# A decoder layer with stick-breaking attention: meta columns in one transpose, first values as a bias, the 528-column scores halved

## The chip, the cores and the metric

The kernel runs on one core of a Trainium2 chip. A core has TensorE (PE; its weight loads are listed apart as PEld), VectorE (DVE), ScalarE (ACT), GpSimd (POOL) and SyncE (SP), whose queue issues nearly all the transfers between device memory (DRAM) and the on-chip memory SBUF. TensorE writes to PSUM, eight banks of 128 partitions by 512 float32 columns; DVE and ACT read it, POOL doesn't in this kernel. Each engine works through its own instructions in order, and the engines wait for each other by semaphores. The metric is the device time of one execution in microseconds.

## The reference

One layer over 2048 tokens and 16 meta tokens in front of them, model width 1024. Every row is normalised and multiplied with one wide weight matrix. The columns feed two kinds of attention, their gates, and a merge:

```
xn   = rms_norm(h, norm_gain)
proj = xn @ w_in            # sb_q, sb_k, sb_v, sw_q, sw_k, sw_v, sb_z, sw_z, g_sb, g_sw
# stick-breaking attention: 8 heads of 64, all earlier positions s < t
z    = q k^T / 8
log_1m = where(mask, log_sigmoid(z) - z, 0)      # log of 1 - sigmoid(z)
w    = where(mask, exp(log_sigmoid(z) + (sum of log_1m over later s)), 0)
o_sb = w v
# sliding-window attention: 16 heads in 2 groups, window 128, a sink per head
o_sw = softmax([scores, sink])[..., :-1] v
y    = sigmoid(g_sb) * ((o_sb * silu(sb_z)) @ w_branch_sb) + sigmoid(g_sw) * ((o_sw * silu(sw_z)) @ w_branch_sw)
out  = rms_norm(h + y @ w_out, final_norm_gain)[:, real tokens]
```

## The kernel before

**Precision.** The result must be that of float32. A float32 value is split in a high part (type fp32r, which TensorE multiplies in one pass) and a low part, the rest; a product is high x high, high x low, low x high, added up in PSUM. So most loops issue three matmuls per block, and the helpers `evac_split` (lines 117 to 120: ScalarE writes the high part at L119, VectorE the low part at L120) and `split` (L110 to L116) occur everywhere.

**Order.** Tokens are in reversed order, 16 blocks of 128, four groups of four blocks (512 columns), two halves: groups 2 and 3 first, then 0 and 1. For each half the kernel computes the stick-breaking q, k and v (`sb_q`, `sb_k`, `sb_v`, kept in DRAM as qd, kd, vd), runs the sliding-window attention (`window`) woven into other projections, then the stick-breaking attention (`stick`) woven into gate projections (L454 are the projections' matmuls). Last comes `finish`, with the output projections. `weave` (L140) takes turns between a main list (projections) and a side list (attention): each `yield` names a cost, and the side may spend `ratio` times what the main has spent. In `stick` the costs are 0.45 for a row, 0.43 for a turn and so on; `cost_sb` (L1388) is their sum and gives the ratio, so that both lists end together.

**Who orders what.** TensorE's instructions go out in the order of the program. The other engines' orders, SP's queue too, are laid down by a planner that simulates the engines beforehand, apart from some stretches at the start that are by hand. At run time each queue is strictly in order.

**Stick-breaking, one row of blocks (`row`, L900).** For a head h and a group g of queries, a step (n, j) takes block j of the group, with 128 queries as partitions, and up to four blocks of keys from block 4(g+n)+j on, up to the last block. Because of the reversal the weights are a running product: a sigmoid of -z by ScalarE (L920), then one scan by VectorE that multiplies along the row (L930; L928 with a mask where the diagonal lies), carried on from the row before. What is kept in a row is the remaining product before each position, so the value matmul uses differences of neighbouring values instead of values (`sb_v`, variable d), and the very first value of each block of queries comes in with weight 1.

Each row that reaches the last key also has 16 columns for the meta tokens. If it has fewer than four blocks, they fit into the same PSUM bank (tag "z", two banks). If it has four (`own`), there are 512 + 16 = 528 scores, and the 16 have a bank of their own (tag "zm", one bank): two matmuls of 512 (L916) and two of 16 (L918), for the two halves of the split q, in the order 512, 16, 512, 16; then two sigmoids (L920, L922). This happens once for each head and group, 32 times.

**Turning (`turn`, L934).** Five or six steps after a row (LT), its 128x128 blocks are transposed by TensorE into a bank "t" (L941), split into wth and wtl (L119, L120), and two steps later multiplied with the value differences vc into the output bank, tag "o", of which there is one (`values`, L967). After the last row of a group, `turn_meta` (L948) transposes the 16 meta columns of each of the four rows, one at a time, into rows 0 to 15 of "zm" (L952), and `evac_split` puts the high part into rows 0 to 15 and the low part into rows 32 to 47 of wm, a constant tile, one for each group of the half. Rows 64 on of wm hold ones at the place of the block they belong to (memset and affine_select, L859 and L860), and the rows of vm against them hold the first values. So one matmul of wm with vm (the last L967 of a group) adds meta tokens and first values. Then ScalarE copies the bank "o" to SBUF (L971) and two DMAs store the result od. Its high and low value columns are stored apart and added later.

**First values (`sb_v`, L547).** The first value of each block is copied to vf (L555); the closure `firsts` transposes eight of them (L578), splits them (L532, L533) and stores them by DMA into vm. The closure `turned` writes the meta values' differences into rows 0 to 15 of vm and copies them to rows 32 to 47 (L596).

Of the kernel before, what the change touches and what calls it, by code (L numbers as in the profile page):

```python
# [11 lines left out]
ALU = mybir.AluOpType  # L12
# [36 lines left out]
def tile_kernel(ctx, tc, x, xt, meta, metat, gain, w_in, w_sb, w_sw, w_out, sinks, fgain,  # L49
# [498 lines left out]
    def sb_v(p):  # L548

        def use(g, acc, ms):  # L550
            t, d = tmp(), tmp()
            A.copy(t, acc)
            V.tensor_tensor(d[:, :GT - 1], t[:, 1:], acc[:, :GT - 1], op=ALU.subtract)
            f0 = p % 2 * 8
            A.copy(vf[:, f0 + g % 2 * 4:f0 + g % 2 * 4 + 4], t.rearrange("p (b q) -> p b q", b=4)[:, :, 0])  # L555

            def join(nxt):
                V.tensor_tensor(d[:, GT - 1:], nxt, t[:, GT - 1:], op=ALU.subtract)
                if g % 2 == 0:
                    A.copy(vn[:, p:p + 1], t[:, 0:1])  # L560

            def rows():
                tr = ps("zm")
                for i in range(4):
                    T.transpose(tr[:, i * P:(i + 1) * P], d[:, i * P:(i + 1) * P], ident)
                hl = tr.rearrange("p (b a d) -> p a b d", b=4, a=2)
                vt = [tmp(F32R).rearrange("p (b d) -> p b d", b=4) for a in range(2)]
                for a, t in enumerate(vt):
                    A.copy(t[:, :, 0:64], hl[:, a])
                for a, t in enumerate(vt):  # L570
                    V.tensor_tensor(t[:, :, 64:128], hl[:, a], f32(t[:, :, 0:64]), op=ALU.subtract)
                for a, t in enumerate(vt):
                    DMA(vd[p][g][a], t)

            def firsts():

                tr = ps("zm")
                T.transpose(tr[:8, :P], vf[:, f0:f0 + 8], ident)  # L578
                vb = tmp(F32R)[:8, :2 * P].rearrange("p (a d) -> p a d", a=2)
                meta_rows(tr[:8, :P], vb[:, :, 0:64], vb[:, :, 64:128])  # L580
                DMA(vm[64 + 4 * g:72 + 4 * g, p], vb)

            def meta():
                mc = meta_cols(ms)
                m = tmp()
                mv, md = m[:, :NM + 1], m[:, 32:32 + NM]
                G.memset(mv[:, NM:], 0.0)
                A.copy(mv[:, :NM], mc)
                V.tensor_tensor(md, mv[:, 1:], mv[:, :NM], op=ALU.subtract)
                join(mv[:, 0:1])  # L590

                def turned():
                    tr = ps("t")
                    T.transpose(tr[:NM, :P], md, ident)
                    meta_rows(tr[:NM, :P], vm[0:NM, p, :, 0:64], vm[0:NM, p, :, 64:128])
                    A.copy(vm[32:32 + NM, p], f32(vm[0:NM, p]))  # L596
                    rows()
                soon.append(turned)

            if ms is None:  # L600
                join(vn[:, p:p + 1] if g % 2 else vf[:, f0 + 4:f0 + 5])
# [246 lines left out]
    def stick(groups, bp):  # L848
# [4 lines left out]
        for tag, shape, n in (("q1", [P, GT], 2), ("q2", [P, GT], 2), ("v", [P, 4, P], 5), ("wh", [P, GT], 3), ("wl", [P, GT], 3),  # L853
                              ("k", [P, KW], 2)):
            for _ in range(n):
                bp.tile(shape, F32R, tag=tag, name=tag, bufs=n)
        for g in groups:
            w = wm[g % 2]
            G.memset(f32(w), 1.0)  # L859
            G.affine_select(out=w, in_=f32(w), pattern=[[-1, 4], [0, P]], compare_op=ALU.is_equal, fill=0.0,  # L860
                            base=-64 - 4 * g, channel_multiplier=1)
        av_todo = []
        mask = None
        if groups[0]:
            mask = bp.tile([P, RW], F32, name="mask")
# [33 lines left out]
        def row(h, g, n, j):  # L899
# [10 lines left out]
            k0 = (b0 - 4 * groups[0]) * P  # L910
            own = end and nb == 4
            z = ps("z")
            zm = ps("zm") if own else None
            for t, qt in enumerate(st["q"]):
                lq = qt[:, j * P:(j + 1) * P]
                T.matmul(z[:, :w], lhsT=lq, rhs=kt[h][:, k0:k0 + w], start=t == 0, stop=t == 1)  # L916
                if own:
                    T.matmul(zm[:, :NM], lhsT=lq, rhs=kt[h][:, k0 + w:k0 + w + NM], start=t == 0, stop=t == 1)  # L918
            r = bp.tile([P, RW], F32, tag="row", name="row", bufs=12)
            A.activation(r[:, :w], z[:, :w], AF.Sigmoid, scale=-1.0)  # L920
            if own:
                A.activation(r[:, w:w + NM], zm[:, :NM], AF.Sigmoid, scale=-1.0)  # L922
                w += NM
            if n == 0 and mask is None:
# [6 lines left out]
            last[j] = r[:, w - 1:w]  # L931
            rows_of[h, g, n, j] = r

        def turn(h, g, n, i):  # L934
# [13 lines left out]
        def turn_meta(h, g):  # L948
            p, a = divmod(h, 2)
            tr = ps("zm")  # L950
            for j in range(4):
                T.transpose(tr[:NM, j * P:(j + 1) * P], rows_of[h, g, 3 - g, j][:, GT - P * j:GT - P * j + NM], ident)  # L952
            w = wm[g % 2]
            evac_split(w[0:NM], w[32:32 + NM], tr[:NM])
            av_todo.append((h, g, vm[:, p, a, :], w, None, False, True))

        def values():
# [10 lines left out]
            if last:  # L968
                p, a = divmod(h, 2)
                u = tmp()  # L970
                A.copy(u, o)  # L971
                for n in range(2):
# [6 lines left out]
        for s in range(n + lt + 3):  # L979
# [4 lines left out]
            if 0 <= t < n:  # L984
# [336 lines left out]
    for half, groups in enumerate(halves):  # L1321
# [61 lines left out]
        with tc.tile_pool(name=f"sb{half}", bufs=1, side="left") as bp:  # L1383
# [106 lines left out]
```

## Time and profile before

| | |
|---|---|
| median of 3 runs | 2112.88 us (2112.0 to 2113.49) |
| the profiled execution | 2112.16 us, span 2110.4 us |
| granted TensorE clock | 0.999 |
| stick-breaking stage, first half | about 374 to 590 us |
| stick-breaking stage, second half | about 1111 to 1612 us |

The profile is of one execution, in microseconds from the first instruction. Its page gives busy time by engine, the chain of work that ended last, and groups of instructions by line: out<-in by the program's names, count, busy time, mean ns of one, and the idle time of the engine just before them with what ended it. A timeline lists instructions in order: start, duration, engine, line, operation, tiles, shape, count. A matmul's listed duration holds its way through the array, so neighbours overlap; what it costs is read from the start of one to the start of the next. A shape such as 128*16 128x128 is the size of the weights and what is streamed past them.

### The profile page before, as it was taken

Reading aid. Unit: us, or ns where it says so; the run is one execution under the profiler, and the core shown is the slowest. Engines: PE = TensorE matmul, PEld = TensorE weight load, DVE = VectorE, ACT = ScalarE, POOL = GpSimd, SP = SyncE. Lnnn points to the kernel's source line nnn. Section 1 sums busy time; section 2 is a strip of 40 time slices with the busy share of each in tenths; the row PEclk is TensorE's granted clock in tenths of the full one; section 3 lists DMA queues with packets and bytes.
Section 4 is the critical chain, followed back from the end, with each engine's and each line's share of the span. In section 5 each row is a group of like instructions: output and inputs, shape, how many; then the busy total and the mean of one; then the engine's idle time right before and its main releaser. Section 6 shows DMA issues by size and latency. Waiting matters only on the chain.

```text
span 2110.4 us, 30845 instructions
## 1 busy us (share of the span) xinstructions
PE 2094.4 (99%) x10695; PEld 1755.2 (83%) x10695; DVE 1479.1 (70%) x2375; ACT 1058.8 (50%) x2438; POOL 300.1 (14%) x484
## 2 busy tenths in 40 slices
PE   9999999999999999999999999999999999999998
PEld 7888888888878888888888888888888888788887
DVE  7897986888878554887738888877774456564553
ACT  6677774555646335777735555555553202221131
POOL 2133444211000000232310000000000232000000
PEclk9999999999999999999999999999999999999999
DMA  9955545766449674435455344343424996568532
GB/s 337 324 174 193 191 168 181 238 194 200 139 142 338 232 256 155 152 136 178 137 172 153 123 126 127 118 125 95 123 88 142 360 323 203 181 232 309 160 100 90
DMA packets 169580, 391.07 MB, mean 185 GB/s; under 512 B 23601, under 2 KB 27697, under 8 KB 169425
## 3 DMA queue, kind: packets, MB, share of 16 engines
q1 hardware_dynamic: 169136, 388.84, 54.9%
q8 instruction: 85, 1.39, 0.3%
q14 instruction: 71, 0.57, 0.1%
q10 hardware_dynamic: 288, 0.27, 0.0%
HBM read 241.68 MB, written 145.18 MB: 183 GB/s over the span
## 4 chain that ended last, share of the span: by engine, by line
PE 91%; DVE 3%; ACT 3%; DMA 2%; issue 1%; SPq 0%; ACTq 0%; DVEq 0%
PE ps_g L454 39%; PE ps_o L967 6%; PE ps_z L916 6%; PE ps_t L941 6%; PE ps_z L754 3%; PE ps_o L810 2%; PE ps_g L252 1%; PE ps_g L253 1%; PE ps_g L251 1%; PE ps_z L252 1%; PE ps_z L251 1%; PE ps_z L253 1%; PE ps_t L252 1%; PE ps_t L253 1%; PE ps_t L251 1%; PE ps_t L788 1%
## 5 line engine op out<-in xcount | busy, mean ns | idle before, releaser
L454 PE MATMUL ps_g<-xh,wh 128*128 128x512 f32 x1296 | 532.1, 411 | 0.8 <-DVE tmp L675 0.5
L454 PE MATMUL ps_g<-xl,wh 128*128 128x512 f32 x1296 | 507.6, 392 | 0.4 <-DVE xl L1169 0.3
L454 PE MATMUL ps_g<-xh,wl 128*128 128x512 f32 x1296 | 507.7, 392 | 0.0
L930 DVE TENSOR_TENSOR_SCAN row<-row 128x512 f32<-128x512 f32 (+4 forms) x256 | 297.1, 1161 | 91.9 <-ACT row L920 39.5
L454 PEld LDWEIGHTS ps_g<-xh,wl 128*128 128x128 f32 x1296 | 243.3, 188 | 54.4 <-DVE wl L1217 0.4
L920 ACT ACTIVATE row<-ps_z 128x512 f32<-128x512 f32 (+1 forms) x320 | 172.4, 539 | 213.5 <-PE ps_z L916 192.3
L454 PEld LDWEIGHTS ps_g<-xh,wh 128*128 128x128 f32 x1296 | 244.3, 188 | 41.4 <-ACT xh L1168 1.0
L454 PEld LDWEIGHTS ps_g<-xl,wh 128*128 128x128 f32 x1296 | 244.8, 189 | 37.8 <-DVE xl L1169 1.7
L119 ACT ACTIVATE wth<-ps_t 128x512 fp32r<-128x512 f32 (+1 forms) x320 | 170.7, 533 | 76.3 <-PE ps_t L941 75.2
L120 DVE SCALAR_TENSOR_TENSOR wtl<-ps_t,wth 128x512 fp32r<-128x512 f32 (+1 forms) x320 | 188.9, 590 | 25.3 <-ACT wth L119 24.8
L916 PE MATMUL ps_z<-kt,q 128*128 128x512 f32 (+3 forms) x640 | 185.3, 369 | 0.0
L941 PE MATMUL ps_t<-ident,row 128*128 128x128 f32 x1088 | 171.7, 273 | 0.1
L941 PEld LDWEIGHTS ps_t<-ident,row 128*128 128x128 f32 x1088 | 134.7, 140 | 34.0 <-DVE wtl L120 1.3
L916 PEld LDWEIGHTS ps_z<-kt,q 128*128 128x128 f32 x640 | 117.9, 188 | 23.5
L967 PE MATMUL ps_o<-wth,vc 128*128 128x512 f32 (+1 forms) x320 | 130.2, 407 | 0.0
L967 PE MATMUL ps_o<-wtl,vc 128*128 128x512 f32 (+1 forms) x320 | 116.3, 363 | 0.0
L762 ACT ACTIVATE sc<-sc,nm 128x129 f32<-128x129 f32 x256 | 100.0, 393 | 27.9 <-DVE nm L760 26.9
L115 POOL TENSOR_SCALAR wh<-raw 128x1024 fp32r<-128x1024 f32 (+1 forms) x47 | 52.8, 1124 | 354.0 <-PE ps_g L454 143.4
L610 ACT ACTIVATE tmp<-ps_g 128x512 f32<-128x512 f32 x84 | 50.3, 598 | 74.1 <-PE ps_g L454 67.0
L925 POOL TENSOR_SCALAR_AFFINE_SELECT row<-row 128x128 f32<-128x128 f32 x64 | 20.4, 318 | 468.2 <-ACT row L920 441.0
L290 ACT CAST ringl<-gt 128x512 fp32r<-128x512 f32 x32 | 19.9, 622 | 129.0 <-DVE gt L288 127.1
L794 POOL TENSOR_SCALAR_AFFINE_SELECT pm<-pl 64x256 fp32r<-64x256 f32 x128 | 74.3, 580 | 37.3 <-DVE pl L120 31.9
(441 smaller groups left out, 4130.1 us busy)
## 6 DMA issues: line engine op xcount, KB each, us to landing
wh<-h_in_w_in SPq DMA_DIRECT2D x66, 512.0 KB, 3.7
wl<-l_in_w_in SPq DMA_DIRECT2D x66, 512.0 KB, 4.9
h_in_w_in<-wh SPq DMA_DIRECT2D x50, 512.0 KB, 3.3
l_in_w_in<-wl SPq DMA_DIRECT2D x50, 512.0 KB, 3.5
raw<-in_w_in SPq DMA_DIRECT2D x49, 512.0 KB, 5.3
q<-qd SPq DMA_DIRECT2D x128, 128.0 KB, 3.3
vc<-vd SPq DMA_DIRECT2D x48, 256.0 KB, 3.1
kd<-tmp SPq DMA_DIRECT2D x32, 256.0 KB, 3.3
```

Of the source, the lines that this page charges most:

```text
L119: A.activation(h, acc, AF.Copy, scale=scale)
L120: V.scalar_tensor_tensor(l, acc, scale, f32(h), op0=ALU.mult, op1=ALU.subtract)
L251: T.matmul(acc, lhsT=wh[:, k, :], rhs=h, start=k == 0, stop=False)
L252: T.matmul(acc, lhsT=wh[:, k, :], rhs=l, start=False, stop=False)
L454: T.matmul(acc, lhsT=a[:, k, :], rhs=b[:, k, :], start=k == i == 0, stop=k == KT - 1 and i == 2)
L762: A.activation(sc[:, hh, :], sc[:, hh, :], AF.Exp, bias=nm[:, hh:hh + 1], accum_out=den[:, hh:hh + 1])
L794: G.affine_select(out=pm[to, :, c], in_=full[r, :, c], pattern=[[0, 4], [sign, HB]], compare_op=ALU.is_ge, fill=0.0, base=n - 1, channel_m ...
L916: T.matmul(z[:, :w], lhsT=lq, rhs=kt[h][:, k0:k0 + w], start=t == 0, stop=t == 1)
L920: A.activation(r[:, :w], z[:, :w], AF.Sigmoid, scale=-1.0)
L930: V.tensor_tensor_scan(r[:, :w], r[:, :w], r[:, :w], last[j] if n else 1.0, op0=ALU.mult, op1=ALU.min)
L941: T.transpose(tr[:, j * P:(j + 1) * P], rows_of[h, g, n - (j > i), j][:, k0:k0 + P], ident)
L967: T.matmul(o[:, :n], lhsT=v, rhs=r, start=first and r is wh, stop=last)
```

## The change

1. `turn_meta`: as soon as a row that reaches the last key is scanned, POOL splits its 16 meta columns into a new tile m, [128, 4 rows, high and low, 16], with a tensor_scalar and a tensor_tensor. One transpose of the whole of m, 128 columns, replaces the four. The bank then has row j's high and low part in rows 32j to 32j+31; four moves of 32 rows by 128 columns, by VectorE and ScalarE in turns, put these into the diagonal blocks of wm, which is zero elsewhere, cleared once at the start. For that, vm holds the meta values eight times over, copied by three DMAs (16, 32, 64 rows), each of which reads what the one before wrote.
2. The first values leave the matmul: `firsts` goes, and POOL copies the first values into the two tiles vfirst, zero in the other head's partitions. ScalarE's copy of "o" becomes four activations (Identity) of 128 columns with the first value of the block as a bias for each partition.
3. The 528 scores are 256 in "z" and 272 in "zm".
4. Row tiles have 640 columns instead of 528, so that each begins at a multiple of 512 bytes; the tile "pad" and the scratch space of DMAs are resized.
5. The weave's costs follow: 0.11 for a `turn_meta` instead of 0.43, 0.33 instead of 0.75 in `cost_sb`.

```diff
-    vf = cp.tile([P, 16], F32, name="vf")
-    cp.tile([P, 40], F32, name="pad")
+    vf = cp.tile([P, 4, 8], F32, name="vf")
+    vfirst = [cp.tile([P, 4, 8], F32, name=f"vf{a}") for a in range(2)]
+    cp.tile([P, 88], F32, name="pad")
...
-    V.memset(f32(vm), 0.0)
+    for t in (*(f32(w) for w in wm), *vfirst):
+        G.memset(t, 0.0)
...
-            def firsts():
-
-                tr = ps("zm")
-                T.transpose(tr[:8, :P], vf[:, f0:f0 + 8], ident)
-                vb = tmp(F32R)[:8, :2 * P].rearrange("p (a d) -> p a d", a=2)
-                meta_rows(tr[:8, :P], vb[:, :, 0:64], vb[:, :, 64:128])
-                DMA(vm[64 + 4 * g:72 + 4 * g, p], vb)
...
-                    A.copy(vm[32:32 + NM, p], f32(vm[0:NM, p]))
+                    for n in (NM, 2 * NM, 4 * NM):
+                        DMA(vm[n:2 * n, p], vm[0:n, p])
...
             if g % 2 == 0:
-                pending.append(lambda: late.append(firsts))
+                for a, t in enumerate(vfirst):
+                    r = slice(64 * a, 64 * a + 64)
+                    G.tensor_copy(t[r, p], vf[r, p])
...
-        for g in groups:
-            w = wm[g % 2]
-            G.memset(f32(w), 1.0)
-            G.affine_select(out=w, in_=f32(w), pattern=[[-1, 4], [0, P]], compare_op=ALU.is_equal, fill=0.0,
-                            base=-64 - 4 * g, channel_multiplier=1)
...
-            own = end and nb == 4
-            z = ps("z")
-            zm = ps("zm") if own else None
+            pieces = [("z", 0, w)]
+            if end and nb == 4:
+                pieces = [("z", 0, w // 2), ("zm", w // 2, w // 2 + NM)]
+                w += NM
+            banks = [ps(tag) for tag, _, _ in pieces]
             for t, qt in enumerate(st["q"]):
-                lq = qt[:, j * P:(j + 1) * P]
-                T.matmul(z[:, :w], lhsT=lq, rhs=kt[h][:, k0:k0 + w], start=t == 0, stop=t == 1)
-                if own:
-                    T.matmul(zm[:, :NM], lhsT=lq, rhs=kt[h][:, k0 + w:k0 + w + NM], start=t == 0, stop=t == 1)
-            r = bp.tile([P, RW], F32, tag="row", name="row", bufs=12)
...
+                for z, (_, c, m) in zip(banks, pieces):
+                    T.matmul(z[:, :m], lhsT=qt[:, j * P:(j + 1) * P], rhs=kt[h][:, k0 + c:k0 + c + m], start=t == 0, stop=t == 1)
+            r = bp.tile([P, 5 * P], F32, tag="row", name="row", bufs=12)
+            for z, (_, c, m) in zip(banks, pieces):
+                A.activation(r[:, c:c + m], z[:, :m], AF.Sigmoid, scale=-1.0)
...
+            if end:
+                if j == 0:
+                    st["m"] = bp.tile([P, 4, 2, NM], F32R, tag="m", name="m", bufs=2)
+                mh, ml = (st["m"][:, j, i, :] for i in range(2))
+                mr = r[:, w - NM:w]
+                G.tensor_scalar(mh, mr, 1.0, 1.0, op0=ALU.mult, op1=ALU.mult)
+                G.tensor_tensor(ml, mr, f32(mh), op=ALU.subtract)
...
+            T.transpose(tr[:, :P], f32(state[h, g]["m"]).rearrange("p j i k -> p (j i k)"), ident)
+            w = wm[g % 2]
             for j in range(4):
-                T.transpose(tr[:NM, j * P:(j + 1) * P], rows_of[h, g, 3 - g, j][:, GT - P * j:GT - P * j + NM], ident)
-            w = wm[g % 2]
-            evac_split(w[0:NM], w[32:32 + NM], tr[:NM])
+                r = slice(32 * j, 32 * j + 32)
+                (V.tensor_copy if j % 2 else A.copy)(w[r, j * P:(j + 1) * P], tr[r, :P])
...
-                A.copy(u, o)
+                for j in range(4):
+                    c = slice(j * P, (j + 1) * P)
+                    A.activation(u[:, c], o[:, c], AF.Identity, bias=vfirst[a][:, p, g % 2 * 4 + j:g % 2 * 4 + j + 1])
...
-                    yield 0.43
+                    yield 0.11
...
-            cost_sb = 8 * sum(4 * (4 - g) for g in groups) * 1.31 + 16 * 0.75 + LT[half] * 0.86
+            cost_sb = 8 * sum(4 * (4 - g) for g in groups) * 1.31 + 16 * 0.33 + LT[half] * 0.86
...
-    nc = bacc.Bacc("TRN2", target_bir_lowering=False, num_devices=1)
+    nc = bacc.Bacc("TRN2", target_bir_lowering=False, num_devices=1, dynamic_dma_scratch_size=1024)
```

More of the change, by code (lines that the diff above doesn't have):

```diff
@@ L553, in use @@
             V.tensor_tensor(d[:, :GT - 1], t[:, 1:], acc[:, :GT - 1], op=ALU.subtract)
-            f0 = p % 2 * 8
-            A.copy(vf[:, f0 + g % 2 * 4:f0 + g % 2 * 4 + 4], t.rearrange("p (b q) -> p b q", b=4)[:, :, 0])
+            A.copy(vf[:, p, g % 2 * 4:g % 2 * 4 + 4], t.rearrange("p (b q) -> p b q", b=4)[:, :, 0])
             def join(nxt):
@@ L600, in use @@
             if ms is None:
-                join(vn[:, p:p + 1] if g % 2 else vf[:, f0 + 4:f0 + 5])
+                join(vn[:, p:p + 1] if g % 2 else vf[:, p, 4:5])
             pending.append(rows if ms is None else meta)
             if g % 2 == 0:
-                pending.append(lambda: late.append(firsts))
+                for a, t in enumerate(vfirst):
+                    r = slice(64 * a, 64 * a + 64)
+                    G.tensor_copy(t[r, p], vf[r, p])
         return weights(C_SBV + p * P), use, "back"
@@ L853, in stick @@
         for tag, shape, n in (("q1", [P, GT], 2), ("q2", [P, GT], 2), ("v", [P, 4, P], 5), ("wh", [P, GT], 3), ("wl", [P, GT], 3),
[L854 removed]
+                              ("k", [P, KW], 2), ("m", [P, 4, 2, NM], 2)):
             for _ in range(n):
                 bp.tile(shape, F32R, tag=tag, name=tag, bufs=n)
[L857 to L861 removed]
         av_todo = []
@@ L864, in stick @@
         if groups[0]:
-            mask = bp.tile([P, RW], F32, name="mask")
+            mask = bp.tile([P, 5 * P], F32, name="mask")
             V.memset(mask[:, P:], 0.0)
```

4 lines of the change are left out of this document (removed).

## The prediction

> **What bounds the kernel now.** I read the page's engine sums, then the chain that ended last, then busy time by stage, then TensorE's order of work.
>
> ```profile
> PE 2094.4 (99%) x10695; PEld 1755.2 (83%) x10695; DVE 1479.1 (70%) x2375; ACT 1058.8 (50%) x2438; POOL 300.1 (14%) x484
> ...
> PE 91%; DVE 3%; ACT 3%; DMA 2%; issue 1%; SPq 0%; ACTq 0%; DVEq 0%
> ```
> ```profile
> 374.00:590.00 216.00, 215.91 (x1215) 182.40 (x1214) 176.74 (x230) 120.21 (x260) 27.99 (x17) 1.00 0.60 185
> ...
> 1111.00:1612.00 501.00, 500.95 (x2721) 419.30 (x2720) 398.61 (x481) 274.63 (x534) 20.37 (x64) 1.00 0.38 116
> ```
>
> The columns of the stages are length, then PE, PEld, DVE, ACT and POOL. TensorE bounds everything; both stick-breaking stages (216 and 501 us) leave it nothing to wait for, at full clock. There is no other work behind which a matmul hides, so each nanosecond of TensorE's queue that goes or comes is one of the span. But busy time misprices it: a 512-column matmul is booked at 0.39 us, while the next starts 0.23 later. So I price by start-to-start distances, and carry them one ordinary matmul further, since a short matmul makes the next one late (its weights aren't loaded yet).
>
> **The scores, 528 in two parts.**
>
> ```profile
> 374.46 0.39 PE L916 MATMUL ps_z<-kt,q 128*128 128x512 f32 x1
> 374.69 0.17 PE L918 MATMUL ps_zm<-kt,q 128*128 128x16 f32 x1
> ...
> 375.37 0.39 PE L454 MATMUL ps_g<-xl,wh 128*128 128x512 f32 x1
> ...
> 376.89 0.41 PE L916 MATMUL ps_z<-kt,q 128*128 128x272 f32 x2
> ...
> 377.37 0.40 PE L454 MATMUL ps_g<-xl,wh 128*128 128x512 f32 x1
> ```
> ```profile
> 252.31 1.11 PE L754 MATMUL ps_z<-kk,q 128*128 128x256 f32 x8
> ...
> 253.49 0.40 PE L454 MATMUL ps_g<-xl,wh 128*128 128x512 f32 x1
> ```
>
> From the first score matmul to the second ordinary one: 375.37 - 374.46 = 0.91, less 0.23 = 0.68 us for 512, 16, 512, 16. Afterwards it is 256, 272, 256, 272. Eight of 256 cost 253.49 - 252.31 - 0.23 = 0.95, so 0.12 each; two of 272 cost 377.37 - 376.89 - 0.23 = 0.25. Together 2 x 0.12 + 0.25 = 0.49. Saved 0.19 on each of 32 rows (8 heads, 4 groups): **6.1 us**. Both sigmoids stay two instructions over the same 528 columns.
>
> **The meta columns, turned at once.**
>
> ```profile
> 388.03 0.60 PE L952 MATMUL ps_zm<-ident,row 128*16 128x128 f32 x4
> ...
> 388.70 0.39 PE L454 MATMUL ps_g<-xl,wh 128*128 128x512 f32 x1
> ```
> ```profile
> 547.01 0.27 PE L941 MATMUL ps_t<-ident,row 128*128 128x128 f32 x1
> 547.12 0.60 PE L952 MATMUL ps_zm<-ident,row 128*16 128x128 f32 x4
> ```
>
> Four transposes cost 388.70 - 388.03 - 0.23 = 0.44. One full transpose is 0.11, whether it loads 16 columns or 128. Three of four go: 0.33 x 32 = **10.5 us**. The eight transposes of first values (L578) go too: 8 x 0.11 = **0.9**. Gross: 17.5 us.
>
> **First values as a bias: the debit.** One copy of the output bank by ScalarE (L971) becomes four activations of 128 columns with a pointer bias. The bank "o" exists once, so the next group's first value matmul waits for all four.
>
> ```profile
> 1493.52 0.39 PE L967 MATMUL ps_o<-wm,vm 128*128 128x512 f32 x1
> ...
> 1495.04 0.47 PE L967 MATMUL ps_o<-wth,vc 128*128 128x512 f32 x1
> 1495.36 0.39 PE L967 MATMUL ps_o<-wtl,vc 128*128 128x512 f32 x1
> ```
> ```profile
> 1495.02 0.19 PEld L967 LDWEIGHTS ps_o<-wth,vc 128*128 128x128 f32 x1
> ```
> ```profile
> 1493.95 0.59 ACT L971 COPY tmp<-ps_o 128x512 f32<-128x512 f32 x1
> 1494.43 0.60 ACT L920 ACTIVATE row<-ps_z 128x512 f32<-128x512 f32 x1
> ```
> ```profile
> L119 ACT ACTIVATE wth<-ps_t 128x128 fp32r<-128x128 f32 x16 | 4.4, 274 | 2.2 <-PE ps_t L941 2.2
> ...
> L113 ACT CAST wh<-raw 128x1024 fp32r<-128x1024 f32 x2 | 2.1, 1048 | 0.4 <-PE ps_g L454 0.4
> ```
> ```profile
> L762 ACT ACTIVATE sc<-sc,nm 128x129 f32<-128x129 f32 x256 | 100.0, 393 | 27.9 <-DVE nm L760 26.9
> ...
> L290 ACT CAST ringl<-gt 128x512 fp32r<-128x512 f32 x32 | 19.9, 622 | 129.0 <-DVE gt L288 127.1
> ```
>
> A 128-column move out of PSUM takes 0.274. A pointer adds: (1048 - 622) / 512 = 0.83 ns a column, so 129 columns without one are 622 - 383 x 0.83 = 304 ns, against 393 for L762, which has one: 0.09. So 0.37 each. Neighbours overlap by 0.11 (L971 ends 1494.54, L920 begins 1494.43), so the fourth ends 3 x 0.26 + 0.37 = 1.15 to 1.18 after the first starts: 1495.12 at best, against 1494.54 now. The weights load that waits for it went at 1495.02. With 0.04 for the hand-over (as from the last value matmul's end, 1493.91, to the copy) the first value matmul comes 0.15 late, 15 times in the second stage: 2.3 us. In the first stage a 528 row always lies in this gap and gets 0.19 shorter.
>
> ```profile
> 393.27 0.40 PE L967 MATMUL ps_o<-wm,vm 128*128 128x512 f32 x1
> ...
> 395.03 0.48 PE L967 MATMUL ps_o<-wth,vc 128*128 128x512 f32 x1
> ```
>
> The gap of 1.76 becomes 1.57, about that of the second stage, with its weights due 0.1 to 0.2 before: 0.2 late, 12 times: 2.4 us. At that stage's last change of group no row is left and the new weave puts the first value 0.45 after the last one (from going through both generators with the new costs): 1.2 us late. Debit **5.9 us**, bounds 0 (four parts as quick as one copy) to 14 (no overlap: 4 x 0.37 ends 0.3 later still). I take the middle because both prices have rows.
>
> The Trainium skill, "ScalarE: Activation LUTs", section "What ACT_TABLE_LOAD costs", gives 93 ns for a pointer operand and 93 for the overlap of neighbours; these rows agree. By its figures alone the four parts take about 1.27 us from SBUF, which would make the debit some 8 us.
>
> **Edits taken at zero, with their cover.** Splitting the 16 columns gives POOL two small operations on 128 end rows, and the transpose now waits for them.
>
> ```profile
> L116 POOL TENSOR_TENSOR wl<-raw,wh 128x1024 fp32r<-128x1024 f32 x7 | 17.8, 2547 | 0.6
> L115 POOL TENSOR_SCALAR wh<-raw 128x1024 fp32r<-128x1024 f32 x7 | 9.1, 1306 | 121.2 <-PE ps_g L454 121.2
> L747 POOL COPY sc<-skb 128x4 f32<-128x4 f32 x32 | 7.9, 254 | 340.0 <-PE ps_t L788 177.9 <-PE ps_g L1099 158.4 <-DVE tmp L775 3.7
> ```
>
> Rows run 5 to 6 steps ahead of their transposes, a step is 501 / 224 = 2.2 us, so about 11 us; scan, two operations of 0.25 and a weight split (3.9) that is in front on POOL fit. Those splits in turn wait behind POOL's wait for a scan; weights are fetched two tiles ahead. The four 32-row moves replace L119 and L120 on 16 rows, 4 us before use. Replicating the meta values is three chained DMAs on SP for each of four head pairs. A small one lands in 2.1 us (xs<-xs), so SP stands up to 6 us a time, and loads and stores behind it with it; bounds 0 to 24 us, taken as 0: SP stands longer now, and TensorE is covered by weights fetched ahead.
>
> ```profile
> xs<-xs SPq DMA_DIRECT2D x32, 64.0 KB, 2.1
> ```
> ```profile
> SPq L59 <- DVE res L304: 86.2, 13, 17.0
> ```
>
> POOL's memsets at the start replace its own and DVE's, before the first weights arrive. Wider rows and moved addresses: 0, bounds -1 to +1, no row of a kind differing by its buffer. The weave's lower costs (0.43 to 0.11, 0.75 to 0.33) follow the shorter work and end the side line 1 us later, at the last main matmul; tail under 0.5 us a stage, in the range.
>
> **Sum.** -6.1 - 10.5 - 0.9 + 5.9 = -11.6 us. The profiled execution took 2112.16 (span 2110.4), 0.7 under the median of 2112.88, so 2101.3 as a median. 0.2% (4.2 us) is about what a measurement of this kernel tells from no change.
>
> **Rivals.** (1) The bank comes free in time and all 17.5 us stay: 2095.4. For it: of those who wait for today's copy the view of L971 names one, once:
>
> ```profile
>   PEld ps_o L967: 0.2, 1
> ```
>
> Against: the spare time is 0.5 us (1495.02 - 1494.54), and the parts need 0.6 more.
> (2) The next row's sigmoid is put among the four parts on ScalarE's in-order queue, adding 0.49. The scores are there some 0.9 us after the last value matmul began, before the fourth part starts, and ScalarE's order already lets others in front of the bank:
>
> ```profile
> 393.47 0.60 ACT L610 ACTIVATE tmp<-ps_g 128x512 f32<-128x512 f32 x1 [0.42 <-PE ps_g L454]
> 393.97 0.58 ACT L971 COPY tmp<-ps_o 128x512 f32<-128x512 f32 x1
> ```
>
> Some 30 x 0.49 = 15 us more: 2116 if always, 2109 if half the time.
> (3) VectorE becomes the bound of the first stage: slower.
>
> ```profile
> 395.16 2.78 DVE L928 TENSOR_TENSOR_SCAN row<-row,mask 128x528 f32<-128x528 f32 x1 [0.36 <-ACT row L922]
> ```
> ```profile
> 394.43 2.39 POOL L116 TENSOR_TENSOR wl<-raw,wh 128x1024 fp32r<-128x1024 f32 x1
> ```
> ```profile
> L930 DVE TENSOR_TENSOR_SCAN row<-row 128x512 f32<-128x512 f32 (+4 forms) x256 | 297.1, 1161 | 91.9 <-ACT row L920 39.5
> ```
>
> A scan, 1.2 us as a rule, took 2.78 beside a POOL subtraction, so each new POOL operation can hold a scan. Room is 216 - 177 = 39 us, less 8 that the stage loses, plus 4 for the smaller meta moves: 35, or 0.55 for each of its 64 end rows; from there on it decides. At 0.9 a pair (two of 0.25, and as much lost around them) it is 58: 23 us over, 2124. At 0.5, which I expect, it stays hidden. The Trainium skill, "SBUF — State Buffer", section "Who interferes with whom", states that a VectorE instruction with two SBUF inputs contends with a GpSimd one that reads SBUF; the row agrees, and the rule speaks against this change.
> (4) The work isn't saved, as one transpose of 128 weight columns costs more than one of 16: the L941 and L952 starts above are 0.11 apart alike, so under 1 in 50.
>
> **Numbers.** Forecast 45%, its own range 2098 to 2105. Rival 1 25%, rival 2 17% (mostly within 0.2%), rival 3 9%, a wait on SP's chain or the like 4%. Faster 77%, same 12%, slower 11%. Leaving out rival 3 and the far end of rival 2: 2094 to 2111.
>
> **What would show it.** L916 as 256 and 272 columns, no L918, next starts 0.12 apart; 32 meta transposes instead of 128; no L578. The debit shows as a wait of the first value's weights load on ScalarE's four bias activations, 0.1 to 0.3 each; POOL some 60 us busier; VectorE's scans longer only in a few places. The prediction is wrong if that wait is absent or above 0.5, if VectorE's share in the first stage nears the whole, or if matmuls of projection wait for weights in the first 370 us.

## The result, and the profile after

| | median | ratio to before, 95% interval |
|---|---|---|
| before, on the same chip | 2111.85 us (2110.71 to 2114.31) | |
| after | 2105.66 us (2104.71 to 2108.62) | 0.9971 (0.9961 to 0.9981) |

The change takes 6.2 us off, 0.29%. The forecast was 11.6, so the direction is right, the time lies in the whole range (2094 to 2111) and just above the forecast's own (2098 to 2105), and about half of the expected gain didn't come. The profiled execution of after has a span of 2105.3 us.

The page of after, engine sums and shares of the chain that ended last:

```profile
PE 2081.7 (99%) x10591; PEld 1745.4 (83%) x10591; DVE 1483.5 (70%) x2398; ACT 1066.6 (51%) x2554; POOL 374.1 (18%) x752
...
PE 89%; DVE 4%; ACT 3%; DMA 2%; issue 1%; SPq 0%; DVEq 0%; POOL 0%; ACTq 0%
```

104 matmuls are gone: 96 meta transposes and 8 of first values. TensorE is still the chain.

Busy time by stage of after (length, then PE, PEld, DVE, ACT, POOL, each with its count):

```profile
374.00:589.00 215.00, 211.63 (x1174) 178.85 (x1173) 178.63 (x249) 124.54 (x321) 68.38 (x143) 1.00 0.61 187
...
1111.00:1607.00 496.00, 495.39 (x2676) 414.55 (x2675) 398.23 (x497) 281.54 (x599) 51.53 (x192) 1.00 0.38 117
```

The second stage is 5 us shorter and TensorE still full (495.4 of 496.0). In the first, 3.4 of 215 us now find TensorE without work, where it was 0.1 of 216 before; counted from the same matmul to the same matmul it is 2.8 us shorter, the second 5.8. So most of what is missing was lost in the first. Who makes it wait is told by the waits of the weights loads, after in the first stage:

```profile
PEld ps_o L964 <- ACT tmp L970: 3.1, 7, 1.3
PEld ps_t L937 <- DVE wtl L122: 1.7, 3, 1.3
PEld ps_o L964 <- DVE wm L951: 1.4, 2, 1.2
```

The same view of before, first stage:

```profile
PEld ps_t L941 <- DVE wtl L120: 0.7, 2, 0.4
PEld ps_o L967 <- ACT tmp L971: 0.2, 1, 0.2
```

The first row of after is the forecast one, the output bank behind the four bias activations (L970). The other two weren't forecast: VectorE's part of the split (L122) later than before, and VectorE's moves of the meta columns into wm (L951).

**The scores, as they came.** The timeline of TensorE in after:

```profile
376.25 0.28 PE L909 MATMUL ps_z<-kt,q 128*128 128x256 f32 x1
376.37 0.29 PE L909 MATMUL ps_zm<-kt,q 128*128 128x272 f32 x1
...
376.61 0.28 PE L909 MATMUL ps_zm<-kt,q 128*128 128x272 f32 x1
376.74 0.40 PE L456 MATMUL ps_g<-xh,wh 128*128 128x512 f32 x1
376.97 0.39 PE L456 MATMUL ps_g<-xl,wh 128*128 128x512 f32 x1
```

By the prediction's own rule, 376.97 - 376.25 - 0.23 = 0.49 us, the figure forecast.

**The bank, as it came.** Second stage of after, ScalarE, then the weights loads, then TensorE:

```profile
1489.91 1.14 ACT L970 ACTIVATE tmp<-ps_o,vf 128x128 f32<-128x128 f32 x4
1491.07 0.60 ACT L912 ACTIVATE row<-ps_z 128x512 f32<-128x512 f32 x1
```
```profile
1491.11 0.19 PEld L964 LDWEIGHTS ps_o<-wth,vc 128*128 128x128 f32 x1
```
```profile
1489.48 0.39 PE L964 MATMUL ps_o<-wm,vm 128*128 128x512 f32 x1
...
1491.11 0.50 PE L964 MATMUL ps_o<-wth,vc 128*128 128x512 f32 x1
```

Four parts take 1.14 us, the next sigmoid comes behind them and not among them, and the weights load goes 0.06 after the last part's end (1491.05). The first value matmul starts 1.63 after the last one of the group before at 13 of the 15 changes of group of this stage, and 2.31 at the other two, where one more block of projections lies between. The view of L970 over the whole kernel, minimum, median and maximum in ns:

```profile
L970 ACT ACTIVATE tmp<-ps_o,vf x128: 359/369/417, 395.0 to 1606.9; 128x128 f32<-128x128 f32 x128
```

One part is 0.369 and four are 4 x 0.369 - 3 x 0.11 = 1.15, as forecast from other rows. (The Trainium skill, "ScalarE: Activation LUTs", "What ACT_TABLE_LOAD costs": 93 ns for a pointer operand; 369 against the 274 of a plain 128-column move is 95, so the row agrees.)

**The meta moves, as they came.** First stage of after, VectorE, then ScalarE, then POOL, then TensorE:

```profile
443.90 0.28 DVE L951 CAST wm<-ps_zm 32x128 fp32r<-32x128 f32 x1
444.22 2.84 DVE L919 TENSOR_TENSOR_SCAN row<-row 128x272 f32<-128x272 f32 x1
447.09 0.30 DVE L951 CAST wm<-ps_zm 32x128 fp32r<-32x128 f32 x1
```
```profile
442.75 0.24 ACT L951 CAST wm<-ps_zm 32x128 fp32r<-32x128 f32 x1
...
444.22 0.26 ACT L951 CAST wm<-ps_zm 32x128 fp32r<-32x128 f32 x1 [0.80 <-DVE wm L951]
```
```profile
444.08 2.40 POOL L118 TENSOR_TENSOR wl<-raw,wh 128x1024 fp32r<-128x1024 f32 x1
```
```profile
446.11 0.27 PE L964 MATMUL ps_o<-wtl,vc 128*128 128x128 f32 x1
447.44 0.51 PE L964 MATMUL ps_o<-wm,vm 128*128 128x512 f32 x1 [1.06 <-DMA zs<-tmp]
```

The four moves write disjoint blocks of one tile, yet they run as a chain: ScalarE 442.75, VectorE 443.90, ScalarE 444.22 (0.80 of it waiting for VectorE's), VectorE 447.09. Each link has to come up in the in-order queue of its engine, and the last one stands behind a scan, which here takes 2.84 us beside POOL's subtraction instead of 0.78 for 272 columns. The value matmul that reads wm starts at 447.44, right after the fourth move ends (447.39). The profile names a DMA for that wait; by the times it is the move. The view of L951, after, shows how general the chain is (idle time of the engine before the moves, by releaser):

```profile
  DVE wm L951: 21.1, 21
  ACT wm L951: 4.2, 13
```

34 of the 128 moves kept an engine idle for the move before them.

**The start.** In this execution the matmuls stand still at 6 to 8 us for data, and from 11 to 14 us they run at half clock:

```profile
12.51 0.63 PE L456 MATMUL ps_g<-xl,wh 128*128 128x512 f32 x1
12.94 0.63 PE L456 MATMUL ps_g<-xh,wh 128*128 128x512 f32 x1
```

Starts are 0.43 apart there instead of 0.23. It costs 2.7 us against before's profile; another execution of the same kernel (a_after, next) lost 0.17 at this place, so it comes and goes with the execution and isn't a cost of the edits. Of the 14 profiles one more has it (a_rows_528, 2.0 us).

### The profile page after: what moved, and what is told of

It is laid out like the page before. It is cut to its first block, busy times and chain, and to the rows that moved or that the text cites. A ratio compares the mean times of both kernels' runs of the same rounds, so it can differ in the third digit from the quotient of the medians.

```text
span 2105.3 us, 31217 instructions
## 1 busy us (share of the span) xinstructions
PE 2081.7 (99%) x10591; PEld 1745.4 (83%) x10591; DVE 1483.5 (70%) x2398; ACT 1066.6 (51%) x2554; POOL 374.1 (18%) x752
## 4 chain that ended last, share of the span: by engine, by line
PE 89%; DVE 4%; ACT 3%; DMA 2%; issue 1%; SPq 0%; DVEq 0%; POOL 0%; ACTq 0%
PE ps_g L456 37%; PE ps_o L964 7%; PE ps_z L909 6%; PE ps_t L937 6%; PE ps_z L750 2%; PE ps_o L806 2%; PE ps_z L456 2%; PE ps_g L255 1%; PE ps_g L253 1%; PE ps_g L254 1%; PE ps_z L255 1%; PE ps_z L253 1%; PE ps_z L254 1%; PE ps_t L255 1%; PE ps_t L253 1%; PE ps_t L254 1%
## 5 line engine op out<-in xcount | busy, mean ns | idle before, releaser
L919 DVE TENSOR_TENSOR_SCAN row<-row 128x512 f32<-128x512 f32 (+4 forms) x256 | 296.9, 1161 | 82.4 <-ACT row L912 42.9
L912 ACT ACTIVATE row<-ps_z 128x512 f32<-128x512 f32 (+2 forms) x320 | 166.0, 519 | 182.9 <-PE ps_z L909 178.2
L122 DVE SCALAR_TENSOR_TENSOR wtl<-ps_t,wth 128x512 fp32r<-128x512 f32 (+1 forms) x320 | 189.7, 593 | 25.3 <-ACT wth L121 23.6
L909 PE MATMUL ps_z<-kt,q 128*128 128x512 f32 (+4 forms) x640 | 178.7, 354 | 0.0
L927 POOL TENSOR_SCALAR m<-row 128x16 fp32r<-128x16 f32 x128 | 29.2, 228 | 415.7 <-DVE row L919 389.0
L790 POOL TENSOR_SCALAR_AFFINE_SELECT pm<-ph 64x256 fp32r<-64x256 f32 x128 | 62.2, 486 | 108.9 <-ACT ph L121 104.8
```

Of the source, the lines that this page charges most:

```text
L122: V.scalar_tensor_tensor(l, acc, scale, f32(h), op0=ALU.mult, op1=ALU.subtract)
L909: T.matmul(z[:, :m], lhsT=qt[:, j * P:(j + 1) * P], rhs=kt[h][:, k0 + c:k0 + c + m], start=t == 0, stop=t == 1)
L912: A.activation(r[:, c:c + m], z[:, :m], AF.Sigmoid, scale=-1.0)
L919: V.tensor_tensor_scan(r[:, :w], r[:, :w], r[:, :w], last[j] if n else 1.0, op0=ALU.mult, op1=ALU.min)
```

## The experiments

Where a stage is credited below, it is by the start of the same projection matmul, counted from the beginning, in two traces: those are the same in all kernels. "Stage 1" is from the matmul at about 365 us in before to that at about 597, "stage 2" from about 1099 to about 1620. Figures are run minus before, in us. The stages are of one profiled execution each; the first two rows are the same kernel twice and show the scatter, 0.2 us within a stage and 1.1 between the stages.

| run | stage 1 | 597 to 794 | stage 2 | whole, medians |
|---|---|---|---|---|
| after | -2.8 | +0.9 | -5.8 | -6.2 |
| a_after | -2.9 | +2.0 | -5.7 | -7.3 |
| a_one_copy | -4.5 | +0.5 | -7.5 | -11.3 |
| a_in_place | -3.9 | -0.1 | -7.4 | -11.1 |
| a_whole_scores | -0.9 | +2.3 | -3.0 | -2.4 |
| b_halves_alone | -2.3 | 0.0 | -2.3 | -4.7 |
| i_m_act_dve | +1.7 | +1.1 | -7.5 | -4.2 |
| i_moves_act | -6.1 | +0.6 | -7.5 | -14.2 |
| i_moves_split | -6.6 | +0.2 | -7.4 | -15.2 |

**The kernel after again, as the base of the comparison (a_after).** No edit.

> The changed kernel again, for the others to stand beside: about 6 us under the kernel before. In the first trace the start cost 2.7 us more than before (the second slice of x landed at 7.8 us and not by 6.0). If that is chance, the start of this trace is like the one before; if the change brings it, matmuls again wait at 6 to 8 us.

2105.38 us, ratio 0.9967 (0.9955 to 0.998). The same waits as above, and in addition one at 747 us, after the transposes of a stretch between the stages, for which the profile names no releaser (timeline of the weights loads):

```profile
747.57 0.19 PEld L456 LDWEIGHTS ps_g<-xh,wh 128*128 128x128 f32 x1 [1.58 <-issue]
```

It is 1.3 to 1.8 us in all five profiles in which the four parts read the bank directly, and 0.2 or nothing in the others; the part on the prediction follows it back to a transfer.

**The bank copied once, the first values left out of the result (a_one_copy).**

```diff
-                for j in range(4):
-                    c = slice(j * P, (j + 1) * P)
-                    A.activation(u[:, c], o[:, c], AF.Identity, bias=vfirst[a][...])
+                A.copy(u, o)
```

> The bank "o" is copied by one instruction again and the first values are left out of the result. Theory of the bank (ScalarE's four parts hold up the next group's first value matmul): the weights load no longer waits, 0.14 us back at some 13 changes of group in the second stage, 0.1 to 0.3 at 13 in the first and 1.2 at its last, 5 us in all: about 2100.5 where the changed kernel has 2105.7. Theory of VectorE (the loss comes from scans that POOL's subtractions hold, and from what stands behind them): no gain, 2105 to 2106.

2101.39 us, 0.9946 (0.9934 to 0.9959), 4.0 us less than a_after. By stages it is 1.7 in stage 2, 1.6 in stage 1, and 1.5 where the wait at 747 is gone; the start and the end of the two profiles differ the other way. So the bank's debit is real, and in the two stages it is 3.3 us. Most of the waits that stay are VectorE's:

```profile
PEld ps_t L937 <- DVE wtl L122: 3.4, 6, 1.3
...
PEld ps_o L964 <- DVE wm L951: 1.5, 2, 1.3
```

With the bank out of the way the wait for wtl grows from 2.5 (a_after) to 3.4: all of that growth is in stage 1, where part of the time that one wait gives back goes into the next.

**The bank copied once, the bias added behind it in SBUF (a_in_place).**

```diff
+                A.copy(u, o)
                 for j in range(4):
                     c = slice(j * P, (j + 1) * P)
-                    A.activation(u[:, c], o[:, c], AF.Identity, bias=vfirst[a][...])
+                    A.activation(u[:, c], u[:, c], AF.Identity, bias=vfirst[a][...])
```

> The bank is copied by one instruction, and the four bias additions follow on the copy in SBUF, in place: same result, 0.6 us more of ScalarE at each of 32 changes. Theory of the bank: as without the additions, 2100.5 to 2101.5, as ScalarE has room (about 57% busy in both stages). Theory of VectorE: 2105 to 2106.

2101.63 us, 0.9951 (0.9938 to 0.9963). ScalarE does the whole work of after and 32 copies more, 18.8 us, and the kernel is 3.75 us faster than a_after: 1.0 in stage 1, 1.7 in stage 2, and the wait at 747 is gone. Stage 1 gives back less than in a_one_copy because the wait on wm grows there, from 1.4 to 2.4. Groups of ScalarE:

```profile
L971 ACT ACTIVATE tmp<-tmp,vf 128x128 f32<-128x128 f32 x128 | 40.9, 400 | 0.3
...
L968 ACT COPY tmp<-ps_o 128x512 f32<-128x512 f32 x32 | 18.8, 586 | 19.7 <-PE ps_o L964 19.1
```

So it isn't ScalarE's time that costs but how long the only output bank is held: 0.59 instead of 1.14 us.

**The change without halved scores (a_whole_scores), and halved scores alone (b_halves_alone).**

```diff
-                pieces = [("z", 0, w // 2), ("zm", w // 2, w // 2 + NM)]
+                pieces = [("z", 0, w), ("zm", w, NM)]
```

The second is the kernel before with its 512 and 16 columns made 256 and 272.

> The 528 scores are 512 and 16 again, all else as changed. The price of the halves by starts is 0.19 us for each of 32 rows, 6.1 us. Theory of VectorE: the whole of it is lost again, about 2111.8. Theory of the bank: in the first stage the 528 row lies in the gap in which the four parts run, so a longer row takes some 2 us of waiting away: about 2109.5.

> The kernel before with one part of the change alone: the 528 scores as 256 and 272. By starts it saves 0.19 us on 32 rows, 6.1 us, with no cost beside it: about 2106.6 where the kernel before has 2112.7. If instead the halves bring waits of their own (the bank "zm" held longer), less than 4 us are left.

2110.32 (0.9989, 0.998 to 0.9998), 4.9 us over a_after; and 2108.17 (0.9977, 0.9969 to 0.9986), 4.7 under before. Both ways the halves are worth 4.7 to 4.9, below the 6.1 forecast. The starts say why for about half of the difference. Of the 32 rows, 16 are followed by a projection matmul and 16 by transposes. Ahead of a projection the 16-column matmul leaves 0.09 us of late weights behind, which the forecast counts as saved. Transposes bring late weights of their own to the next projection matmul; measured to there, these rows save 0.15 instead of 0.19 (512, 16, 512, 16 with two transposes 0.86 us in before, 0.71 with the halves). 16 x 0.193 + 16 x 0.152 = 5.5. The last 0.7 isn't placed.

**The meta columns split by ScalarE and VectorE instead of POOL (i_m_act_dve), on a_in_place.**

```diff
-                G.tensor_scalar(mh, mr, 1.0, 1.0, op0=ALU.mult, op1=ALU.mult)
-                G.tensor_tensor(ml, mr, f32(mh), op=ALU.subtract)
+                A.copy(mh, mr)
+                V.tensor_tensor(ml, mr, f32(mh), op=ALU.subtract)
```

> The kernel with the additions in place (2101.6), and the meta columns split by ScalarE and VectorE instead of POOL. If POOL's two small operations are what holds VectorE in the first stage, the waits of 1 to 1.4 us at 443 and 469 us go: about 2099. If they come from POOL's subtraction of a weight split (2.4 us, it holds the scan beside it), they stay: 2101 to 2102, with more work on VectorE (128 small operations of 0.15 us, 20 us).

2108.65, 0.9979 (0.997 to 0.9988): 7 us worse than a_in_place, 5.6 of it in stage 1; neither of the two expected outcomes. The wait on the bank comes back, with one ScalarE copy:

```profile
PEld ps_o L964 <- ACT tmp L968: 4.6, 7, 1.7
...
PEld ps_o L964 <- DVE wm L951: 2.5, 3, 1.2
```
```profile
422.16 0.20 ACT L927 CAST m<-row 128x16 fp32r<-128x16 f32 x1 [2.45 <-DVE row L919]
422.27 0.58 ACT L968 COPY tmp<-ps_o 128x512 f32<-128x512 f32 x1
```

The second fence is ScalarE's timeline at the longest of these waits. ScalarE's small copy has to wait for the scan (L919), and the bank's copy stands behind it in the queue; it is the same at all seven. POOL isn't the trouble that rival 3 made of it; of the two places tried for these operations it is the better one.

**All four meta moves on ScalarE (i_moves_act on a_in_place, a_moves_act on after).**

```diff
-                (V.tensor_copy if j % 2 else A.copy)(w[r, j * P:(j + 1) * P], tr[r, :P])
+                A.copy(w[r, j * P:(j + 1) * P], tr[r, :P])
```

> The kernel with the additions in place (2101.6), and all four moves into wm on ScalarE, none on VectorE. If the wait for wm at 443 us comes from the second move standing behind a held scan on VectorE's in-order queue, the wait of the last value matmul on VectorE (4.4 us for its engine over the run, 5 times) goes, and with it 1 to 2.5 us of time: about 2100. The wait at 469 us, which is on wtl, stays.

> The changed kernel with one edit: all four moves into wm on ScalarE; the bias additions still come straight from the bank. If the wait for wm behind VectorE's scan and the wait for the bank are two separate costs, this gains about the 3 us that it gained on top of the additions in place: 2102.5. If the moves gain only where the bank is free early, nothing: 2105.5.

2098.7, 0.9933 (0.9921 to 0.9946), some 2.9 under a_in_place, 2.2 of it in stage 1. In the view of L951 nothing stands any more under who waited for it:

```profile
L951 ACT CAST wm<-ps_zm x128: 237/256/262, 388.5 to 1597.1; 32x128 fp32r<-32x128 f32 x128
...
who waited for it (us, times):
```

On after itself the same line gives 2103.99, 0.996 (0.9948 to 0.9973), between the two outcomes expected: 1.4 under a_after (1.0 if each is set against the kernel before of its own series), and 1.3 in stage 1. There the bank still stands behind it (4.0 us of waits on L970), and the wait at 747 is 1.8. The intervals of a_moves_act and a_after overlap; that the wait on wm is gone from its trace is certain, the 1.4 isn't.

**Is it POOL that holds VectorE's scans? (i_split_act_dve, on a_in_place)** In stage 1 the splits of weights go to ScalarE and VectorE, so that no POOL subtraction runs beside a scan.

```diff
-            hsplit[0] = vsplit[0] = False
+            hsplit[0] = vsplit[0] = True
```

> The kernel with the additions in place (2101.6), and the seven weight splits of the first stick-breaking stage on ScalarE and VectorE instead of POOL. If the scans are held by POOL's subtractions of weights (11 us of VectorE's time in that stage), both waits of the first stage go: 2.5 to 3 us, about 2099. VectorE takes 7 x 1.2 us more itself, ScalarE 7 x 1.05. If POOL's small operations hold it, nothing changes.

2101.67, 0.9945 (0.9933 to 0.9957): nothing. The same place as above, VectorE, then TensorE:

```profile
441.65 0.28 DVE L951 CAST wm<-ps_zm 32x128 fp32r<-32x128 f32 x1
441.97 0.78 DVE L919 TENSOR_TENSOR_SCAN row<-row 128x272 f32<-128x272 f32 x1
442.78 0.69 DVE L122 SCALAR_TENSOR_TENSOR wtl<-ps_t,wth 128x512 fp32r<-128x512 f32 x1
443.39 0.51 DVE L919 TENSOR_TENSOR_SCAN row<-row 128x144 f32<-128x144 f32 x1
443.93 0.30 DVE L951 CAST wm<-ps_zm 32x128 fp32r<-32x128 f32 x1
```
```profile
444.29 0.50 PE L964 MATMUL ps_o<-wm,vm 128*128 128x512 f32 x1 [1.28 <-DVE wm L951]
```

The scan takes its 0.78 now, and TensorE waits 1.28 all the same, since two scans and a split lie between VectorE's two moves. So the long scan beside POOL, the striking line of the trace, isn't needed for this wait; the chain through VectorE's queue is enough. The edit isn't a clean test of everything that a held scan costs, since the splits are now work of ScalarE and VectorE themselves: in stage 1 the waits for wtl fall from 2.0 to 0.6 us against a_in_place, and those on wm rise from 2.4 to 3.0 and those on the bank from 0.7 to 1.6.

**Both together (i_moves_split): a_in_place, moves on ScalarE, splits on ScalarE and VectorE.**

> Additions in place and moves on ScalarE (2098.7), and the seven weight splits of the first stage on ScalarE and VectorE. What waited for VectorE with the moves gone is wtl, behind a scan that POOL's subtraction of weights held: 0.9 us at 468 us and 0.4 at 492. If that holding is the cause, about 1 us less, 2097.5; if VectorE's queue is simply full, the same 2098.7.

2097.16, 0.9929 (0.9915 to 0.9943), the fastest of all: 15.2 us under before, 8 under after. It isn't told apart from i_moves_act by the intervals; the step between them by stage is 0.5. The waits left of those that the change had brought:

```profile
PEld ps_t L937 <- DVE wtl L122: 1.7, 2, 1.0
PEld ps_o L964 <- ACT tmp L968: 1.6, 3, 0.7
```

**The old costs in the weave (i_costs_before, on i_moves_act), and row tiles of 528 (a_rows_528, on after).**

```diff
-                    yield 0.11
+                    yield 0.43
...
-            cost_sb = 8 * sum(4 * (4 - g) for g in groups) * 1.31 + 16 * 0.33 + LT[half] * 0.86
+            cost_sb = 8 * sum(4 * (4 - g) for g in groups) * 1.31 + 16 * 0.75 + LT[half] * 0.86
...
-            mask = bp.tile([P, 5 * P], F32, name="mask")
+            mask = bp.tile([P, RW], F32, name="mask")
...
-            r = bp.tile([P, 5 * P], F32, tag="row", name="row", bufs=12)
+            r = bp.tile([P, RW], F32, tag="row", name="row", bufs=12)
```

> Additions in place and moves on ScalarE (2098.7), with the weave's costs as before (0.43 a turn_meta, 0.75 in the sum). The order of TensorE's work is then that of the kernel before, and the last change of group in the first stage gets 0.7 us more room: the wait of 0.7 us at 573 us goes, about 2098. If the new costs are worth more than that, by better spacing, it is slower than 2099.5.

> The changed kernel with row tiles of 528 columns again, so that they begin at differing multiples of 64 bytes. I priced the wider rows at zero: 2105.4, between 2104.5 and 2106.5. If the common begin matters, scans, sigmoids or weights loads of rows change their durations (1.22, 0.60, 0.14 us).

2097.42, 0.9929 (0.9916 to 0.9941), against 2098.7 with the new costs: no difference that can be told, and if any, the new costs are the worse ones. The wait on the bank at the last change of group of stage 1 went from 0.7 to 0.2 us, as expected. The 528-wide tiles give 2106.6, 0.9971 (0.9961 to 0.9982), the ratio of after to the last digit. The scans' group of that run, all shapes together, 1157 ns each against 1161 in after:

```profile
L919 DVE TENSOR_TENSOR_SCAN row<-row 128x512 f32<-128x512 f32 (+4 forms) x256 | 296.1, 1157 | 82.5 <-ACT row L912 43.0 <-POOL row L914 36.8
```

## Why the prediction was right and wrong

**Right: the bound and the prices by starts.** With TensorE full in both stages, matmuls taken away are time taken away. Once most of the waits are gone (i_moves_split), the two stages give back 6.6 and 7.4 of some 8.0 each that the starts promise. Halved scores at 0.49 and a full transpose at 0.11 (0.115 measured) came as read, and where the neighbouring matmuls are the same in both kernels at least three times, one transpose in place of four takes 0.33 less. Rival 4 is out.

**Right in its mechanism, too large in size: the bank.** Four parts of 0.37 overlapped to 1.14, with the weights load behind them. What they cost is the difference between a_after and a_one_copy from the last value matmul of a group to the second projection matmul after the next group's first value. In stage 2 it is 0.12 to 0.14 us at 13 of the 15 changes (forecast 0.15 at all 15) and nothing at the two that have one more block of projections between: 1.6 us where 2.3 was forecast, and 1.7 came back. In stage 1 it is 2.3 where 3.6 was forecast: 0.55 at the last change and about 0.1 at most others, where 0.2 was forecast. The wait at that last change is 1.25 us in after (forecast 1.2), but 0.7 of it stays with one copy (0.2 in before, and 0.2 with the old costs of the weave): that part is the price of the new order and not of the four parts. The other waits that the profile names on the bank are about 0.3 us, one 0.5. Of the 2.3 only 1.0 to 1.6 came back. The first stage has other late work right behind, and a wait removed there is partly taken over by the next. Rival 1 (the bank free in time) is refuted, and rival 2 too: at none of the 32 changes is another instruction of ScalarE put among the parts.

**Wrong in size: the scores,** 6.1 forecast, 5.5 by starts, 4.7 to 4.9 measured. The step that failed is "carry them one ordinary matmul further": it was read at rows followed by projections and applied to all 32, half of which are followed by transposes. That is 0.6 of the 1.2 to 1.4 that are missing; the rest is open.

**Wrong: "the four 32-row moves replace L119 and L120 on 16 rows, 4 us before use", taken at zero.** The lead of 4 us was right (the transpose at 442.05, the value matmul due at 446.4), and the four moves by themselves are about 1.1 us. But they go by turns on two engines and run one after the other, so the lead must also hold the work that lies between VectorE's two moves in its queue. Moved to one engine they keep nobody waiting: 2.9 us back with the bank settled, about 1.4 without. The prediction said itself that what is queued in front counts, for POOL's splits; for these moves it didn't ask.

**Rival 3, refuted in its place.** POOL is busier by 74 us (60 forecast), and VectorE's busy time in stage 1 went from 176.7 to 178.6: the operations of 128x16 don't hold the scans. In after the 13 scans of 272 columns beside such an operation take 0.73 us in the median, the 17 with no work on POOL beside them 0.78. Groups of after:

```profile
L928 POOL TENSOR_TENSOR m<-row,m 128x16 fp32r<-128x16 f32 x128 | 45.4, 355 | 10.0
L927 POOL TENSOR_SCALAR m<-row 128x16 fp32r<-128x16 f32 x128 | 29.2, 228 | 415.7 <-DVE row L919 389.0 <-DVE row L917 23.8 <-PE ps_t L937 0.7
```

The Trainium skill's rule ("SBUF — State Buffer", "Who interferes with whom") agrees with the scan of 2.84 us beside a 1024-column subtraction; beside operations of 16 columns no such hold was seen. VectorE as a source of waits was in the rival, but through a queue and not through its load.

**Right at zero:** the three chained DMAs on SP's queue (2.1 to 2.9 us in the median from issue to landing, no matmul held by them), wider rows and, but for that last change of group, the weave's costs.

```profile
vm<-vm SPq DMA_DIRECT2D x4, 64.0 KB, 2.9
...
vm<-vm SPq DMA_DIRECT2D x4, 32.0 KB, 2.1
```

**The sum again.** Forecast -17.5 + 5.9. By the runs: the gross is about 16.9 by starts (scores 5.5); the bank takes 2.7 to 3.3 in the two stages (1.7 and 1.0 to 1.6); the moves take 1.4 to 2.9; the wait at 747 takes 1.3 to 1.6. That leaves -9 to -11.5, against -6.2 to -7.3 measured. The rest, 2 to 5, isn't placed: 1.7 of the gross come back in no variant (15.2 in i_moves_split), and single waits of about a microsecond between the stages come and go from one kernel to the next. That the time still lies in the range is partly luck: the bank cost less than was forecast, and this made up in part for the moves and the wait at 747, which weren't in the sum.

**Not in the sum: the wait at 747 us.** It is there in all five profiles with the four parts on the bank and in none of the other nine, though the last change of group lies some 160 us earlier. In all 14 traces the weights load goes 0.07 to 0.10 us after VectorE has copied the bank "g" out (L1102 in a_after). In the five VectorE is late there, because it stood before for a transfer. VectorE in a_after:

```profile
744.35 0.75 DVE L425 SCALAR_TENSOR_TENSOR xs<-xs,gn,rb 128x512 f32<-128x512 f32 x1 [1.67 <-DMA xs<-in_xt]
...
746.82 0.68 DVE L1102 TENSOR_TENSOR tmp<-ps_g,tmp 128x512 f32<-128x512 f32 x1
```

This transfer of xs landed 4.1 to 4.6 us after its issue in the five, and 2.6 to 2.9 in the nine. With it goes one packet of 16 KB on a queue that the profile calls "instruction" (the DMA view of a_after, 737 to 746 us):

```profile
q8 instruction: 1, 0.02, 0.9%
```

In the five such a packet starts 1.5 to 2.1 us after the issue of the transfer and takes 0.9 to 1.3 us, while the transfer is under way. In the nine none starts from 7 us before the issue to 8 us after it. A long issue on SP's queue just before, 1.36 us in a_after, isn't the cause: in a_moves_act the same issue takes 0.38, and the wait is the longest, 1.81. That the packet is what delays the transfer is read from five profiles against nine; no run moved it, and why these five kernels have it at that moment stays open.

## What to carry to other kernels

When several engines write parts of one tile in turns, cost the hand-over as a chain through each of their in-order queues, not as a sum of durations, and put all parts on one engine if nothing else speaks against it. If a PSUM bank exists once and the next matmuls are waiting for it, release it with one plain copy and do the rest from SBUF: here that was more work for ScalarE and 2.7 us less in the two stages. And when a wait is named, ask what is late next: where several are stacked, as in the first stage here, only part of a removed wait comes back as time. A wait without a releaser can be followed by hand: look for the last thing in other engines that ends at a fixed distance before it in every trace.

## What the runs showed of the hardware

A 16-column matmul between longer ones makes the next projection matmul about 0.09 us late, and a transpose in between does so itself, so the price of a short matmul depends on what follows it: 0.19 or 0.15 us saved by the same edit. Splitting 16 columns on POOL costs about 0.2 to 0.36 us an operation and left the scans beside it alone (0.73 us for 272 columns against 0.78), while a 1024-column subtraction made a scan of 272 columns last 2.84 us instead of 0.78. After an early stall the first matmuls ran at half clock in two of the 14 profiles: a start distance of 0.43 us for some 3 us, and in after the profile's clock column at 0.50 from 12 to 14 us. What decides it wasn't tried. A transfer during which a 16 KB packet of the queue "instruction" ran landed 4.1 to 4.6 us after its issue in five profiles, and 2.6 to 2.9 us after it in the nine without one.
